# A two-layer hybrid trunk on one core: last states left out, transposed token factors, an ordered end, and sums of squares in two exact passes

## The chip, the cores and the metric

The kernel runs on one core of a Trainium2 chip. The metric is the device time of one execution in microseconds (us). Engines: PE does the matmuls and transposes, DVE and ACT the elementwise work, POOL a few masks, SP issues most transfers.

## What is computed

Two pre-norm residual layers over 1024 tokens of 1024 features, and a last norm. Layer 0 mixes with a convolution branch and an mLSTM with four heads, layer 1 with gated linear attention (GLA), and each is followed by a SwiGLU FFN.

```python
def rmsnorm(x, g):
    return x * rsqrt(mean(x * x, -1) + EPS) * g

def reference(x, ...):
    for l in range(2):
        h = rmsnorm(x, mix_norm_g[l])
        x = x + (conv_mlstm_mixer(h, ...) if l % 2 == 0 else gla_mixer(h, ...))
        h = rmsnorm(x, ffn_norm_g[l])
        x = x + (silu(h @ w1[l]) * (h @ w3[l])) @ w2[l]
    return rmsnorm(x, final_norm_g)

# both recurrent mixers go over chunks of tokens; a chunk reads the state and then renews it
# mLSTM: S = (q k') * decays;  h = (S v + q C) / max(|...|);  C, n = decay * (C, n) + (wk' v, sum wk)
# GLA:   o = A v + (q exp(b)) S;                              S = exp(a) * S + (k exp(a - b))' v
# the convolution branch ends in silu(layernorm(u))
```

## The kernel before

Features lie on the partitions, in 8 tiles of 128, and tokens on the free axis, in two halves of 512. Every large product is `mm3` (L156): both operands are split into a high part, rounded to fp32r, and the rest, also fp32r (`split`, L136: a copy on ACT, L137, and a subtraction on DVE, L138; L152 and L153 do the same for weights in `weights`), and three passes on PE (L158 low weights or low data, L159, L160) make up one fp32 product. The FFN's products are done with seven instead of eight block products, named T1 to T4 and B11 to B22. PSUM has four banks of the tag "mm" and four of "sm".

The instructions on each engine are put in order by a scheduler, when the program is built, from the order of the code and from priorities; `behind(a, b)` (L140) makes a come after b on its engine. In the first mixer the code is emitted in the order of the list `ORDER0`: "a3a" is the preparation (`head_pre`) of head 3 on the first half, "x2b" the mix (`head_mix`) of head 2 on the second half, and so on.

`rstd_half` (L180) makes the reciprocal root of a norm: eight squares on ACT (L185), seven additions on DVE (L187) into `s`, one fp32 matmul with a matrix of 1/1024 (`ones_d`, L189) that sums over the partitions and leaves the result in all of them, and `rsqrt` (ACT L171, DVE L172 to L174). It is called eleven times: twice in the first mixer (`factors`, which also wants the factor of each token on a partition, `rc`: four matmuls of one column, L196, and a second `rsqrt`), after each output projection (twice per layer), after each FFN (L205 then scales), and three times in `finish`, whose last two calls are for 256 tokens each.

`head_pre` loads two rows by SP (`rb`, `wb`), makes the scores (L557), transposes the keys of four chunks (L561), and makes `rb`, `q` and `kw` on DVE (L567, L568, L570). `head_mix` goes over the chunks: L585 the state's increment, L586 and L588 the output, L591 or L594 the new state, L604 the evacuation. In the layer norm of the convolution branch (`layer_norm`, `mean`) four matmuls of 128 columns (L394) add up and sum. In GLA, L799 transposes the keys, L852 makes the increment, L853 and L855 the output, L860 the new state.

The last product, B22, is done in two pieces of 256 tokens. In the second piece the passes go unit by unit (two of the 22 blocks of the inner dimension), the last `LASTU` = 2 units together. L1231 adds the four banks to the residual, and `finish` follows: L1307 scales and L1308 writes out.

Of the kernel before, what the change touches and what calls it, by code (L numbers as in the profile page):

```python
# [29 lines left out]
ORDER0 = ['c0', 'g0', 'c1', 'c2', 'q0', 'c3', 'a0a', 'v0', 'x0a', 'v1', 'x0b', 'g1', 'q1', 'a1a', 'v2', 'x1a', 'v3', 'x1b', 'l', 'g2', 'q2', 'a2a', 'q3', 'x2a', 'x2b', 'a3a', 'n3', 'g3', 'x3a', 'a3b', 'x3b', 'k0', 'n1a', 'n1b']  # L30
# [29 lines left out]
LASTU = 2  # L60
YK = 2
# [11 lines left out]
def trunk_kernel(ctx, tc, xT, cols, gate_b0, ev_vo0, ev_u, ev_cw, ev_out, od_v0, od_u, od_out, gate_w2,  # L73
# [39 lines left out]
    POOL.memset(ones_d, 1.0 / D)  # L113
    epsc = cp.tile([P, 1], F32, tag="epsc", name="epsc")
# [41 lines left out]
    def mm3(o, lt, rt, start, stop, on=False):  # L156

        PE.matmul(o, lt[1], rt[0], start=start and not on, stop=False, skip_group_check=on)  # L158
        PE.matmul(o, lt[0], rt[1], start=False, stop=False, skip_group_check=on)  # L159
        PE.matmul(o, lt[0], rt[0], start=False, stop=stop, skip_group_check=on)  # L160
# [16 lines left out]
    stat = ["sm"]  # L177
    order = [list(range(KT))]

    def rstd_half(xs, r=None, rc=None):  # L180
        n = xs[0].shape[1]
        s = tp.tile([P, HALF], F32, tag="s", name=nm("s"), bufs=1)[:, :n]
        for j, k in enumerate(order[0]):
            q = tmp()[:, :n] if j else s
            ACT.activation(q, xs[k], AF.Square)  # L185
            if j:
                DVE.tensor_tensor(out=s, in0=s, in1=q, op=ALU.add)  # L187
        b = bank(stat[0])[:, :n]
        PE.matmul(b, ones_d, s, start=True, stop=True)  # L189
# [3 lines left out]
        if rc is not None:  # L193
            b = bank("sm")[:, :4]
            for c in range(4):
                PE.matmul(b[:, c:c + 1], s[:, c * P:(c + 1) * P], ones_d[:, 0:1], start=True, stop=True)  # L196
            rsqrt(rc, b)
# [67 lines left out]
    def mixer0(cut, then):  # L265
        with tc.tile_pool(name="m0", bufs=1, reuse_waits="tile") as mp:
# [125 lines left out]
            def mean(b, s):  # L392
                for e in range(4):
                    PE.matmul(b, ones_p, s[:, e * NT:(e + 1) * NT], start=e == 0, stop=e == 3)  # L394
# [151 lines left out]
            def head_pre(hd, half, q, k):  # L546
# [12 lines left out]
                for c in range(4):  # L559
# [4 lines left out]
                for c in range(4):  # L564
# [5 lines left out]
                DVE.tensor_tensor(out=kw.rearrange("p (c t) -> p c t", c=4),  # L570
                                  in0=kb.rearrange("p (c t) -> p c t", c=4),
                                  in1=wk[:, half * 4:half * 4 + 4, hd:hd + 1].to_broadcast([P, 4, P]), op=ALU.mult)
                return q, rb, wb, kw

            def head_mix(hd, half, pre, v, og, st):
                q, rb, wb, kw = pre
                em = gcols["em"]
                for c2 in range(2):
                    db = bank("sm").rearrange("p (c x) -> p c x", c=2)
                    nb = bank("sm").rearrange("p (c x) -> p c x", c=2)  # L580
                    for cc2 in range(2):
# [3 lines left out]
                        PE.matmul(db[:, cc2, :129], kw[:, cs], v[half][:, c, :], start=True, stop=True)  # L585
# [3 lines left out]
                        new = mp.tile([P, 129], F32, tag=f"st{hd % 2}", name=nm("st"), bufs=2)  # L589
                        if st is None:  # L590
                            DVE.tensor_copy(new, db[:, cc2, :129])  # L591
                        else:
# [78 lines left out]
    def mixer1(h, cut, then):  # L671
        y = [[None, None] for _ in range(KT)]
        with tc.tile_pool(name="m1", bufs=1, reuse_waits="tile") as mp:
# [109 lines left out]
            def head_mix(hd, half, q, k, v, st):  # L783
# [8 lines left out]
                kt = tmp()  # L792
                kt3 = kt.rearrange("p (c t) -> p c t", c=4)
# [643 lines left out]
```

## Time and profile before

| | |
|---|---|
| median of 3 runs | 2171.84 us (2170.99 to 2172.52) |
| the profiled execution | 2171.36 us, its span 2169.6 us |
| PE busy | 2152.9 us, 99% |
| DVE busy | 1545.4 us, 71% |
| ACT busy | 866.3 us, 40% |
| granted clock of PE, mean | 0.998 |

The span is what the profiler saw of the program; the execution's own time has 1.76 us around it. A busy PE is not a PE at its peak: records of pipelined matmuls overlap, so the pace of a group is taken from the starts of its first and last instruction. In rows of the timeline the brackets give the idle time of the engine before a row, and what ended it.

### The profile page before, as it was taken

The page shows a single profiled execution, that of the slowest core. Times are in us where ns is not written, and L with a number is a line of the kernel's source. Part 1 is how long each engine was busy: PE and PEld are TensorE (multiplying, and loading weights), DVE is VectorE, ACT ScalarE, POOL GpSimd, SP SyncE. Part 2 cuts the span into 40 slices and gives each one's busy share as a digit, 9 for nine tenths or more (in the row PEclk, how much of TensorE's full clock was granted, in tenths as well). Part 3 has the DMA queues.
Part 4 walks back from the last instruction along what each step waited for, and adds up shares of the span by engine and source line. Part 5 has one row for each costly group of instructions (what it writes and reads, how often), then busy time and mean ns, then how long its engine had stood idle before and what let it go on. Part 6 is the DMA issues. An engine that isn't in the chain of part 4 may idle for free.

```text
span 2169.6 us, 28952 instructions
## 1 busy us (share of the span) xinstructions
PE 2152.9 (99%) x10854; PEld 1830.4 (84%) x10854; DVE 1545.4 (71%) x2585; ACT 866.3 (40%) x1419; POOL 20.8 (1%) x56
## 2 busy tenths in 40 slices
PE   9999999999999999999999999999999999999998
PEld 8889988888888888888889989888888888888887
DVE  7555788777776666867866747587877666667687
ACT  6302327443222323444564534454522222235553
POOL 0000000000000000000110000000000000000000
PEclk9999999999999999999999999999999999999999
DMA  4233453654442336535311011154544333274344
GB/s 167 79 125 111 135 136 117 208 181 170 164 139 95 107 109 211 199 117 165 120 54 40 21 48 31 38 160 170 194 147 165 135 107 107 88 265 157 98 122 131
DMA packets 137979, 278.49 MB, mean 128 GB/s; under 512 B 22320, under 2 KB 35504, under 8 KB 137840
## 3 DMA queue, kind: packets, MB, share of 16 engines
q1 hardware_dynamic: 136688, 275.61, 39.0%
q8 instruction: 85, 1.39, 0.3%
q10 hardware_dynamic: 1152, 1.05, 0.1%
q14 instruction: 54, 0.44, 0.1%
HBM read 209.99 MB, written 66.62 MB: 127 GB/s over the span
## 4 chain that ended last, share of the span: by engine, by line
PE 95%; DVE 3%; ACT 1%; issue 0%; DMA 0%; SPq 0%; DVEq 0%; ACTq 0%
PE mm L158 20%; PE mm L160 20%; PE mm L159 20%; PE sm L159 9%; PE sm L160 9%; PE sm L158 9%; PE sm L382 2%; PE sm L835 1%; PE sm L852 1%; PE sm L853 1%; PE sm L855 1%; PE sm L189 0%; DVE wL L153 0%; PE sm L808 0%; ACT hH L137 0%
## 5 line engine op out<-in xcount | busy, mean ns | idle before, releaser
L159 PE MATMUL mm<-hL,wH 128*128 128x512 f32 x1420 | 555.6, 391 | 0.5 <-DVE hL L310 0.5
L160 PE MATMUL mm<-hH,wH 128*128 128x512 f32 x1420 | 555.3, 391 | 0.0
L158 PE MATMUL mm<-hH,wL 128*128 128x512 f32 x1420 | 520.7, 393 | 1.4 <-DVE wL L153 0.9
L158 PEld LDWEIGHTS mm<-hH,wL 128*128 128x128 f32 x1420 | 266.4, 188 | 58.0 <-DVE wL L153 1.8
L159 PEld LDWEIGHTS mm<-hL,wH 128*128 128x128 f32 x1420 | 266.7, 188 | 55.8 <-DVE hL L310 1.1
L160 PEld LDWEIGHTS mm<-hH,wH 128*128 128x128 f32 x1420 | 266.7, 188 | 54.8
L159 PE MATMUL sm<-hL,wH 128*128 128x512 f32 x616 | 240.5, 390 | 0.0
L160 PE MATMUL sm<-hH,wH 128*128 128x512 f32 x616 | 239.7, 389 | 0.0
L158 PE MATMUL sm<-hH,wL 128*128 128x512 f32 x616 | 209.3, 390 | 0.0
L137 ACT ACTIVATE wH<-S 128x1024 fp32r<-128x1024 f32 x88 | 93.3, 1060 | 212.7 <-PE sm L160 212.7
L137 ACT ACTIVATE wH<-q 128x512 fp32r<-128x512 f32 x143 | 90.4, 632 | 180.4 <-PE mm L160 100.0
L138 DVE TENSOR_TENSOR wL<-q,wH 128x512 fp32r<-128x512 f32 x143 | 98.5, 689 | 73.8 <-ACT wH L137 73.3
L159 PE MATMUL mm<-wL,hH 128*128 128x256 f32 (+2 forms) x512 | 145.8, 286 | 0.0
L160 PE MATMUL mm<-wH,hH 128*128 128x256 f32 (+2 forms) x512 | 145.4, 286 | 0.0
L158 PE MATMUL mm<-wH,hL 128*128 128x256 f32 (+2 forms) x512 | 144.5, 286 | 0.6 <-DVE xy L1231 0.6
L159 PEld LDWEIGHTS sm<-hL,wH 128*128 128x128 f32 x616 | 115.6, 188 | 24.9 <-issue 1.0
L158 PEld LDWEIGHTS sm<-hH,wL 128*128 128x128 f32 x616 | 115.6, 188 | 24.5 <-PE mm L160 0.5
L160 PEld LDWEIGHTS sm<-hH,wH 128*128 128x128 f32 x616 | 115.6, 188 | 24.5 <-issue 0.5
L152 ACT ACTIVATE wH<-raw 128x1024 fp32r<-128x1024 f32 (+2 forms) x77 | 81.6, 1059 | 113.9 <-PE mm L160 84.7
L138 DVE TENSOR_TENSOR wL<-S,wH 128x1024 fp32r<-128x1024 f32 x88 | 107.4, 1220 | 23.9 <-ACT wH L137 23.9
L1040 DVE TENSOR_TENSOR c<-sm,c 128x512 f32<-128x512 f32 x110 | 75.5, 687 | 66.1 <-PE sm L160 66.1
L153 DVE TENSOR_TENSOR wL<-raw,wH 128x1024 fp32r<-128x1024 f32 (+2 forms) x77 | 94.1, 1222 | 38.7 <-ACT wH L152 38.7
(301 smaller groups left out, 3722.2 us busy)
## 6 DMA issues: line engine op xcount, KB each, us to landing
raw<-in_w SPq DMA_DIRECT2D x108, 512.0 KB
mdT<-c SPq DMA_DIRECT2D x88, 256.0 KB
m<-mdT SPq DMA_DIRECT2D x88, 256.0 KB
mdB<-c SPq DMA_DIRECT2D x66, 256.0 KB
q<-in_w SPq DMA_DIRECT2D x60, 256.0 KB
m<-mdB SPq DMA_DIRECT2D x55, 256.0 KB
xsp<-xy SPq DMA_DIRECT2D x48, 256.0 KB
raw<-in_od_u SPq DMA_DIRECT2D x22, 512.0 KB
```

Source lines behind the costliest of these rows:

```text
L137: ACT.activation(dst[0], src, AF.Copy)
L138: return lo.tensor_tensor(out=dst[1], in0=src, in1=dst[0], op=ALU.subtract)
L152: ACT.activation(hi, raw, AF.Copy)
L153: lo.tensor_tensor(out=low, in0=raw, in1=hi, op=ALU.subtract)
L158: PE.matmul(o, lt[1], rt[0], start=start and not on, stop=False, skip_group_check=on)
L159: PE.matmul(o, lt[0], rt[1], start=False, stop=False, skip_group_check=on)
L160: PE.matmul(o, lt[0], rt[0], start=False, stop=stop, skip_group_check=on)
L382: PE.matmul(o, w[:, m * P:(m + 1) * P], raw[:, e, m:m + NT], start=m == 0, stop=m == SH)
L835: PE.matmul(lb[:, j * P:(j + 1) * P], X[:, 2 * j * P:(2 * j + 1) * P], X[:, (2 * j + 1) * P:(2 * j + 2) * P], start=True, stop=True)
L852: PE.matmul(db[:, cc, :], kw[:, cs], v[:, c, :], start=True, stop=True)
L853: PE.matmul(ob[:, cc, :], A[:, cs], v[:, c, :], start=True, stop=st is None)
L1040: DVE.tensor_tensor(out=out, in0=a, in1=b, op=ALU.add)
```

## The change

- `PARTS`: five of the nine sums of squares over 512 tokens (the second of `factors`, the first of layer 0's output projection, both after layer 0's FFN, the first of layer 1's output projection) split `s` (ACT copy, DVE subtraction) and take two fp32r passes with `ones_r`, a copy of `ones_d`, since 1/1024 has no low part.
- `rc`: the result `r`, alike in all partitions, is transposed four times on PE, and one DVE copy takes a column of each.
- `mean`: two additions on DVE (256 and 128 wide) and one matmul, in place of four matmuls; twice.
- Last states: the last chunk of a sequence renews its state for nobody. Its key transposes, increments and state updates are left out in both mixers, four heads each.
- `ORDER0`: "a3a" goes ahead of "x2b", and "a3b" ahead of "x3a".
- Ordered end: in the last two units of the last piece the passes are chained, so that a bank has its nine passes in a row. The scalings of the first piece (`spread`) are put behind later units (`QK` = 6 on). In the last call of `rstd_half` the last square isn't added on DVE: PE sums `s` and that square in two fp32 matmuls.

```diff
-ORDER0 = [..., 'x2a', 'x2b', 'a3a', 'n3', 'g3', 'x3a', 'a3b', 'x3b', 'k0', 'n1a', 'n1b']
+ORDER0 = '... x2a a3a x2b n3 g3 a3b x3a x3b k0 n1a n1b'.split()
+QK = 6
+PARTS = (1, 2, 4, 5, 6)
+    ones_r = cp.tile([P, P], F32R, tag="ones_r", name="ones_r")
+    ACT.activation(ones_r, ones_d, AF.Copy)
...
     def rstd_half(xs, r=None, rc=None):
...
-            if j:
+            if j and (j < KT - 1 or not stat[1]):
                 DVE.tensor_tensor(out=s, in0=s, in1=q, op=ALU.add)
         b = bank(stat[0])[:, :n]
-        PE.matmul(b, ones_d, s, start=True, stop=True)
+        if n < HALF or len(sums) not in PARTS:
+            PE.matmul(b, ones_d, s, start=True, stop=not stat[1])
+            if stat[1]:
+                PE.matmul(b, ones_d, q, start=False, stop=True)
+        else:
+            p = tmp(F32R), tmp(F32R)
+            split(p, s, DVE)
+            PE.matmul(b, ones_r, p[1], start=True, stop=False)
+            PE.matmul(b, ones_r, p[0], start=False, stop=True)
+        sums.append(s)
...
         if rc is not None:
-            b = bank("sm")[:, :4]
+            b = bank("sm")
             for c in range(4):
-                PE.matmul(b[:, c:c + 1], s[:, c * P:(c + 1) * P], ones_d[:, 0:1], start=True, stop=True)
-            rsqrt(rc, b)
+                PE.transpose(b[:, c * P:(c + 1) * P], r[:, c * P:(c + 1) * P], ident)
+            DVE.tensor_copy(rc, b.rearrange("p (c t) -> p c t", c=4)[:, :, 0])
...
             def mean(b, s):
-                for e in range(4):
-                    PE.matmul(b, ones_p, s[:, e * NT:(e + 1) * NT], start=e == 0, stop=e == 3)
+                for n in (2 * NT, NT):
+                    DVE.tensor_tensor(out=s[:, :n], in0=s[:, :n], in1=s[:, n:2 * n], op=ALU.add)
+                PE.matmul(b, ones_p, s[:, :NT], start=True, stop=True)
...
# head_pre of the first mixer; the product kw is n chunks wide too
-                for c in range(4):
+                n = 4 - half
+                for c in range(n):
                     PE.transpose(kb[:, cs], k[:, cs], ident)
...
# head_mix of the first mixer
-                        PE.matmul(db[:, cc2, :129], kw[:, cs], v[half][:, c, :], start=True, stop=True)
+                        more = ci < 7
+                        if more:
+                            PE.matmul(db[:, cc2, :129], kw[:, cs], v[half][:, c, :], start=True, stop=True)
...
-                        else:
+                        elif more:
                             DVE.scalar_tensor_tensor(out=new, in0=st, scalar=wb[:, te:te + 1], ...)
...
# head_mix of GLA: kt, kb and kw have n = 4 - half chunks, and
-                        PE.matmul(db[:, cc, :], kw[:, cs], v[:, c, :], start=True, stop=True)
+                        if c < n:
+                            PE.matmul(db[:, cc, :], kw[:, cs], v[:, c, :], start=True, stop=True)
...
-                        else:
+                        elif c < n:
                             DVE.scalar_tensor_tensor(out=new, in0=st, scalar=ea[:, c:c + 1], ...)
...
# ffn_down
-                            if (name == "B22" or name == "T1" and ks[0] >= SK) and spread:
+                            if (name == "B22" and (not c0 or ks[0] >= QK) or name == "T1" and ks[0] >= SK) and spread:
                                 for ins in spread.pop(0):
                                     behind(ins, low)
+                        if final and c0 and ks[-1] == N - 1:
+                            while spread:
+                                for ins in spread.pop(0):
+                                    behind(ins, low)
...
+                    prev = []
                     for i in range(4):
                         for k, w, m in g:
-                            mm3(banks[i], wcol(w, i, P), m, k == 0, k == N - 1, on)
+                            ins = mm3(banks[i], wcol(w, i, P), m, k == 0, k == N - 1, on)
+                            if len(us) > 1:
+                                for m_ in ins:
+                                    if prev:
+                                        behind(m_, prev[-1])
+                                    prev = [m_]
...
-                    stat[0] = "sm" if half else "mm"
+                    stat[:] = "sm" if half else "mm", final and c0 > 0
```

Where instructions stand: rows of one engine in program order, with the line, the operation and out<-in by the program's names. Line numbers of the kernel after are larger (L162 to L164 are the three passes, L606, L607 and L609 are L585, L586 and L588, L643 is L622).

PE at the first sum of the first mixer, before (`mm_...` are the input projections):

```order
L159 MATMUL mm_272<-hL_40_181,wH_120 128x512
L160 MATMUL mm_272<-hH_39_180,wH_120 128x512
L189 MATMUL sm_208<-s_185,ones_d 128x512
L196 MATMUL sm_215<-ones_d,s_185 128x1 x4
L334 MATMUL sm_265<-e_263 128x128
L159 MATMUL mm_326<-hL_55_227,wH_117 128x512
```

After; the transposes of `rr` stand 46 passes behind the sum:

```order
L164 MATMUL mm_270<-hH_39_182,wH_122 128x512
L196 MATMUL sm_210<-s_187,ones_d 128x512
L163 MATMUL mm_324<-hL_54_225,wH_119 128x512
L164 MATMUL mm_324<-hH_53_224,wH_119 128x512
...
L163 MATMUL mm_349<-hL_68_253,wH_122 128x512
L164 MATMUL mm_349<-hH_67_252,wH_122 128x512
L212 MATMUL sm_217<-ident,rr_186 128x128 x4
L350 MATMUL sm_263<-e_261 128x128
L162 MATMUL mm_442<-wH_425,hL_26_155 128x264
```

The token factors moved from directly behind the sum to the end of the following projections, in front of the small matmul of L350 (L334 before).

PE at the end of head 3 in the first mixer, before; `uw` are weights of the next stage's product, `mm_3478` an output projection:

```order
L160 MATMUL mm_3580<-hH_541_3416,uw_3574 128x512
L561 MATMUL sm_3328<-ident,qk_2895 128x128 x4
L585 MATMUL sm_3342<-v_3053,kw_3340 128x129
L586 MATMUL sm_3343<-v_3053,rb_3319 128x129
L588 MATMUL sm_3343<-st_3307,qk_2859 128x129
L586 MATMUL sm_3343<-v_3053,rb_3319 128x129
L585 MATMUL sm_3364<-v_3053,kw_3340 128x129
L586 MATMUL sm_3365<-v_3053,rb_3319 128x129
L585 MATMUL sm_3342<-v_3053,kw_3340 128x129
L588 MATMUL sm_3343<-st_3347,qk_2859 128x129
L588 MATMUL sm_3365<-st_3352,qk_2859 128x129
L586 MATMUL sm_3365<-v_3053,rb_3319 128x129
```

After, with head 3's second preparation some 50 rows earlier:

```order
L574 MATMUL sm_3265<-qk_2848,qk_2884 128x128 x4
L579 MATMUL sm_3270<-ident,qk_2884 128x128 x3
L606 MATMUL sm_3283<-v_3037,kw_2956 128x129
L162 MATMUL mm_3459<-hH_525_3367,wL_3454 128x512
...
L609 MATMUL sm_3305<-st_3309,qk_2776 128x129
L607 MATMUL sm_3327<-v_3038,rb_3261 128x129
L609 MATMUL sm_3327<-st_3314,qk_2848 128x129
L607 MATMUL sm_3327<-v_3038,rb_3261 128x129
L606 MATMUL sm_3348<-v_3038,kw_3281 128x129
L606 MATMUL sm_3326<-v_3038,kw_3281 128x129
L609 MATMUL sm_3327<-st_3331,qk_2848 128x129
L607 MATMUL sm_3349<-v_3038,rb_3261 128x129
```

The transposes moved ahead of the products of the next stage; the row of small matmuls at the end now has the first half's last chunk in it and no product between.

PE at the end of the kernel, before; `mm_18474` to `mm_18477` are the four banks:

```order
L158 MATMUL mm_18477<-hH_3414_18611,q_18403 128x256
L159 MATMUL mm_18474<-hL_3415_18612,q_18403 128x256
L160 MATMUL mm_18474<-hH_3414_18611,q_18403 128x256
L159 MATMUL mm_18475<-hL_3415_18612,q_18403 128x256
L160 MATMUL mm_18475<-hH_3414_18611,q_18403 128x256
L159 MATMUL mm_18476<-hL_3415_18612,q_18403 128x256
L160 MATMUL mm_18476<-hH_3414_18611,q_18403 128x256
L159 MATMUL mm_18477<-hL_3415_18612,q_18403 128x256
L160 MATMUL mm_18477<-hH_3414_18611,q_18403 128x256
L189 MATMUL sm_18678<-s_18655,ones_d 128x256
```

After, the last bank and the sum:

```order
L162 MATMUL mm_18462<-hH_3411_18590,q_18351 128x256
L163 MATMUL mm_18462<-hL_3412_18591,q_18351 128x256
L164 MATMUL mm_18462<-hH_3411_18590,q_18351 128x256
L162 MATMUL mm_18462<-hH_3411_18590,q_18355 128x256
...
L163 MATMUL mm_18462<-hL_3415_18597,q_18388 128x256
L164 MATMUL mm_18462<-hH_3414_18596,q_18388 128x256
L196 MATMUL sm_18662<-s_18640,ones_d 128x256
L198 MATMUL sm_18662<-t_18660,ones_d 128x256
```

The last two passes of each bank moved in front of the next bank's passes, and the sum is two matmuls.

DVE ahead of that, before (`hL_3415` is the low half of the last operand):

```order
L1307 SCALAR_TENSOR_TENSOR xy_3004_16787<-xy_3004_16787,col,r_18452 128x256
L1307 SCALAR_TENSOR_TENSOR xy_3066_17039<-xy_3066_17039,col,r_18452 128x256
L1307 SCALAR_TENSOR_TENSOR xy_3068_17043<-xy_3068_17043,col,r_18452 128x256
L1307 SCALAR_TENSOR_TENSOR xy_3070_17047<-xy_3070_17047,col,r_18452 128x256
L1307 SCALAR_TENSOR_TENSOR xy_3072_17051<-xy_3072_17051,col,r_18452 128x256
L187 TENSOR_TENSOR s_18655<-s_18655,t_18663 128x256
L138 TENSOR_TENSOR hL_3415_18612<-m_18609,hH_3414_18611 128x256
L1231 TENSOR_TENSOR xy_2998_16775<-xy_2998_16775,mm_18474 128x256
L1231 TENSOR_TENSOR xy_3000_16779<-xy_3000_16779,mm_18475 128x256
L1231 TENSOR_TENSOR xy_3002_16783<-xy_3002_16783,mm_18476 128x256
L1231 TENSOR_TENSOR xy_3004_16787<-xy_3004_16787,mm_18477 128x256
L187 TENSOR_TENSOR s_18655<-s_18655,t_18666 128x256
```

After:

```order
L1341 SCALAR_TENSOR_TENSOR xy_3004_16772<-xy_3004_16772,col,r_18437 128x256
L193 TENSOR_TENSOR s_18640<-s_18640,t_18648 128x256
L142 TENSOR_TENSOR hL_3415_18597<-m_18594,hH_3414_18596 128x256
L1341 SCALAR_TENSOR_TENSOR xy_3066_17024<-xy_3066_17024,col,r_18437 128x256
L1341 SCALAR_TENSOR_TENSOR xy_3068_17028<-xy_3068_17028,col,r_18437 128x256
L1341 SCALAR_TENSOR_TENSOR xy_3070_17032<-xy_3070_17032,col,r_18437 128x256
L1341 SCALAR_TENSOR_TENSOR xy_3072_17036<-xy_3072_17036,col,r_18437 128x256
L1265 TENSOR_TENSOR xy_2998_16760<-xy_2998_16760,mm_18459 128x256
L1265 TENSOR_TENSOR xy_3000_16764<-xy_3000_16764,mm_18460 128x256
L193 TENSOR_TENSOR s_18640<-s_18640,t_18651 128x256
L1265 TENSOR_TENSOR xy_3002_16768<-xy_3002_16768,mm_18461 128x256
L193 TENSOR_TENSOR s_18640<-s_18640,t_18654 128x256
L193 TENSOR_TENSOR s_18640<-s_18640,t_18657 128x256
```

The low half moved ahead of four scalings, and the squares' sums stand between the adds of the banks.

More of the change, by code (lines that the diff above doesn't have):

```diff
@@ L156, in mm3 @@
     def mm3(o, lt, rt, start, stop, on=False):
-        PE.matmul(o, lt[1], rt[0], start=start and not on, stop=False, skip_group_check=on)
-        PE.matmul(o, lt[0], rt[1], start=False, stop=False, skip_group_check=on)
-        PE.matmul(o, lt[0], rt[0], start=False, stop=stop, skip_group_check=on)
+        return (PE.matmul(o, lt[1], rt[0], start=start and not on, stop=False, skip_group_check=on),
+                PE.matmul(o, lt[0], rt[1], start=False, stop=False, skip_group_check=on),
+                PE.matmul(o, lt[0], rt[0], start=False, stop=stop, skip_group_check=on))
     def wcol(w, k, c):
@@ L791, in head_mix @@
                 DVE.tensor_tensor(out=qt, in0=qt, in1=q, op=ALU.mult)
[L792 to L794 removed]
+                n = 4 - half
+                kt = tmp()[:, :n * P]
+                kt3 = kt.rearrange("p (c t) -> p c t", c=n)
+                DVE.tensor_tensor(out=kt3, in0=b3[:, :n, P - 1:P].to_broadcast([P, n, P]), in1=b3[:, :n], op=ALU.subtract)
                 ACT.activation(kt, kt, AF.Exp, scale=1.0 / 16)
[L796 to L798 removed]
+                DVE.tensor_tensor(out=kt, in0=kt, in1=k[:, :n * P], op=ALU.mult)
+                kb = bank("sm")[:, :n * P]
+                for c in range(n):
                     PE.transpose(kb[:, c * P:(c + 1) * P], kt[:, c * P:(c + 1) * P], ident)
[L800 removed]
+                kw = mp.tile([P, HALF], F32, tag="kw", name=nm("kw"), bufs=1)[:, :n * P]
                 ACT.activation(kw, kb, AF.Copy)
```

22 lines of the change are left out of this document (9 added, 13 removed).

## The prediction

> **What bounds the kernel now.** I read the head of the page first, then the chain of waits, then the stretches of the timeline that the edits touch.
>
> ```profile
> span 2169.6 us, 28952 instructions
> PE 2152.9 (99%) x10854; PEld 1830.4 (84%) x10854; DVE 1545.4 (71%) x2585; ACT 866.3 (40%) x1419; POOL 20.8 (1%) x56
> PEclk9999999999999999999999999999999999999999
> PE 95%; DVE 3%; ACT 1%; issue 0%; DMA 0%; SPq 0%; DVEq 0%; ACTq 0%
> ```
>
> PE is busy 99% of the span and carries 95% of the chain, and its clock is at 9 in every slice. So nearly everywhere a matmul taken away shortens the run by its own pace, unless DVE or ACT then becomes late. Two places differ: the last 12 us, where PE waits for the last norm, and the first mixer, where DVE is nearly as full as PE. The sum is made against the profiled execution, which took 2171.36 us (1.76 us around its span); the median of the three runs, 2171.84, stands 0.48 above it.
>
> **Prices.** The pieces of the chain in order of time give what an instruction costs when PE is the bound. The columns are start, length, what, and number of records; an fp32 matmul leaves two records, an fp32r pass or a transpose one.
>
> ```profile
> 243.67 0.44 PE sm L561 x4
> 256.96 0.89 PE sm L394 x8
> 876.80 0.91 PE mm L158 x4
> 1088.42 0.86 PE sm L189 x2
> 1159.45 0.44 PE sm L799 x4
> 1179.77 0.43 PE sm L852 x2
> ```
>
> - Sums of squares: one fp32 matmul 512 wide is 0.86; an fp32r pass of that width is 0.91/4 = 0.227, two are 0.455. Five sums: 5 x (0.86 - 0.455) = 2.0 us less.
> - Factors of the tokens:
>
> ```profile
> 19.42 1.02 PE L189 MATMUL sm<-s,ones_d 128*128 128x512 f32 x2
> 20.28 0.95 PE L196 MATMUL sm<-ones_d,s 128*128 128x1 f32 x8
> 21.15 0.48 PE L334 MATMUL sm<-e 8*128 8x128 f32 x2
> ```
>
> From the start of the four one-column matmuls to the next is 21.15 - 20.28 = 0.87; four transposes are 0.44 (row 243.67). Twice: 0.9 us less.
> - Mean and variance of the layer norm: four accumulating matmuls, 0.89, become one, 0.22: twice 0.67 = 1.3 us less.
> - Last states: 4 transposes of L561 at 0.11 = 0.44; 4 matmuls of L585 at 0.22 (taken as L394, 128 against 129 columns) = 0.89; 4 transposes of L799 at 0.11 = 0.44; 4 matmuls of L852 at 0.43 = 1.7.
>
> Together 7.7 us of PE. Of these 3.9 lie in the first mixer (one sum 0.4, factors 0.9, mean 1.3, L561 0.4, L585 0.9), and 3.8 outside (four sums 1.6, GLA 2.1).
>
> **Outside the first mixer.** The state updates that go there free DVE as well, so 2.1 passes whole. Each split sum puts a copy and a subtraction between the added squares and PE: 1.3 us by 24 splits that have 512 columns too.
>
> ```profile
> L138 DVE TENSOR_TENSOR hL<-t,hH 128x512 fp32r<-128x512 f32 x24 | 15.9, 681 | 0.0
> L137 ACT ACTIVATE hH<-t 128x512 fp32r<-128x512 f32 x24 | 15.0, 627 | 1.3 <-DVE t L205 1.1
> ```
>
> The tightest of the four is the sum at 1088.42, where the second half of layer 1 waits for it.
>
> ```profile
> 1092.46 3.40 DVE L205 SCALAR_TENSOR_TENSOR t<-xy,col,r 128x512 f32<-128x512 f32 x5
> 1098.09 0.60 PE L739 MATMUL sm<-ident,glc 128*128 128x128 f32 x4
> ```
>
> PE has 9.7 us of other matmuls from that sum to row 1098.09, and DVE starts the scaling at 1092.46; a scale that comes 1.2 later can cost between 0 and 1.2. I take 0: in the new order the two passes stand behind 13 more matmuls of the first half (1.6 us), and 39 are left between them and the work that needs the norm. If this cover were gone, the late one would be the subtraction that feeds the second half's first projection. The copy of the constant (ACT, once, at the start) falls where ACT waits for the first weights: nothing.
>
> **The end.** Rows by engine, with the idle time and its releaser in brackets:
>
> ```profile
> 2147.43 0.60 PE L189 MATMUL sm<-s,ones_d 128*128 128x256 f32 x2
> 2153.90 0.42 DVE L138 TENSOR_TENSOR hL<-m,hH 128x256 fp32r<-128x256 f32 x1
> 2157.45 0.28 PE L160 MATMUL mm<-hH,q 128*128 128x256 f32 x1
> 2157.05 1.41 DVE L1231 TENSOR_TENSOR xy<-xy,mm 128x256 f32<-128x256 f32 x4 [2.74 <-PE mm L160]
> 2158.39 2.00 DVE L187 TENSOR_TENSOR s<-s,t 128x256 f32<-128x256 f32 x4
> 2157.57 1.41 ACT L185 ACTIVATE t<-xy 128x256 f32<-128x256 f32 x4 [6.58 <-DVE xy L1231]
> 2160.45 1.22 PE L189 MATMUL sm<-s,ones_d 128*128 128x256 f32 x2 [2.71 <-DVE s L187]
> 2161.70 0.47 ACT L171 ACTIVATE r<-sm,epsc 128x256 f32<-128x256 f32 x1 [2.73 <-PE sm L189]
> ```
>
> And two windows (us, busy PE, PEld, DVE, ACT, POOL, granted clock, DMA share, GB/s):
>
> ```profile
> 2157.00:2160.00 3.00, 0.73 (x7) 0.53 (x5) 2.63 (x8) 1.41 (x4) 0.00 (x0) 0.96 0.00 0
> 2160.00:2162.00 2.00, 1.22 (x2) 0.51 (x2) 0.39 (x1) 0.30 (x1) 0.00 (x0) 0.50 0.00 0
> ```
>
> Before, the four banks are finished 0.24 apart, so four adds, four squares and four sums form a tail of 3 us (2157.45 to 2160.45). Afterwards each bank takes its nine matmuls in a row, 9 x 0.12 = 1.08 us, so banks 0 to 2 are added, squared and summed under PE. After the last matmul there remain: the third bank's sum, which DVE has queued ahead of the last add (it ends near 2158.1: bank 2 done 1.08 earlier, then 0.32 to its add, 0.52 to its square, 0.47 to its sum, each with its length); the last add; its square 0.52 later, 0.42 long; then PE's second matmul near 2159.1. That is 1.35 earlier. DVE must have the last low half (row 2153.90) before PE's eighth matmul of the row of 36 rather than its 29th: that is due near 2154.1, and in the new order only four of the eight scalings stand ahead of it instead of all eight, so it ends near 2152.7. If that failed, PE would wait 0.2 at most by the old time.
>
> The second piece of the gain is the clock. The last sum takes 1.22 at a granted clock of 0.50, and the same shape at 2147.43 takes 0.60. PE had stood still 2.71 us. With two matmuls in place of one, PE pauses only some 0.4 us before each, so I take 0.60: 0.6 us more. Low end: 0 (the clock drops anyway); the first of the two matmuls is hidden, since the last square is ready only later. The end gives 2.0 us, at least 1.3. By the Trainium skill ("TensorE: Matmul & The Clock Gate", Part 1) the clock follows how busy the PE has recently been over a window of about 3.4 us; no row here measures that length, and by it a pause of 0.4 us could not halve the clock.
>
> **The first mixer.** Windows of 20 us, then PE's waits in the last of them, then two DVE rows ahead of the first wait:
>
> ```profile
> 280.00:300.00 20.00, 20.00 (x97) 16.77 (x95) 19.15 (x33) 5.20 (x6) 0.00 (x0) 1.00 0.35 96
> 330.00:350.00 20.00, 20.00 (x164) 19.61 (x163) 19.00 (x42) 19.94 (x37) 0.00 (x0) 1.00 0.28 81
> 350.00:370.00 20.00, 17.88 (x108) 15.22 (x107) 16.91 (x41) 10.88 (x36) 0.00 (x0) 1.00 0.47 142
> ```
>
> ```profile
> 351.89 0.49 PE L585 MATMUL sm<-v,kw 128*128 128x129 f32 x2 [0.70 <-DVE st L591]
> 353.02 0.50 PE L158 MATMUL mm<-hH,wL 128*128 128x512 f32 x1 [0.42 <-DVE wL L153]
> 364.56 0.49 PE L585 MATMUL sm<-v,kw 128*128 128x129 f32 x2 [0.78 <-DVE kw L570]
> 366.84 0.49 PE L588 MATMUL sm<-st,qk 128*128 128x129 f32 x2 [0.22 <-DVE st L594]
> ```
>
> ```profile
> 349.30 2.08 DVE L138 TENSOR_TENSOR hL<-xy,hH 128x512 fp32r<-128x512 f32 x2
> 351.55 0.28 DVE L591 COPY st<-sm 128x129 f32<-128x129 f32 x1
> ```
>
> PE can run ahead of DVE only by what DVE has free: 0.85 us in the window from 280, 1.00 in that from 330, together 1.85. What is saved behind 350 us (half of L561 and L585, 0.66) meets a DVE that has 3 us free. So of 3.9 us 1.85 + 0.66 = 2.5 pass. DVE's own work hardly changes: 1.4 us of narrow adds at most (four, each no longer than the 0.35 of an add 256 wide in row 2157.05), 0.7 for a split, against four state updates of 0.28 and six operations of the second reciprocal root taken out.
>
> The new order puts head 3's preparation (its two row loads on SP, the scores, transposes, exponentials and DVE's three products) ahead of head 2's second mix. That takes the wait for kw (0.78) away, since some 50 passes then lie between kw's product and its use, and leaves other work between the first matmuls of head 3's first half, where PE now waits 0.70 for a state copy queued behind a split of 2.08. PE is idle 20.00 - 17.88 = 2.1 us there. Its bounds: 2.1 gained, or 2.1 lost, if the preparation delays a split by as much as the split in row 349.30 delays the state. The loads cost nothing with a DMA share of 0.28. I take 1.0 gained: the two waits for head 3's state are replaced by a bare row of 14 small matmuls at the end, in which matmul, state update and next matmul follow one another; row 366.84 shows such a link waiting 0.22, and four or five links are 1 us.
>
> **Sum.** Outside 3.8, end 2.0, first mixer 2.5, waits 1.0: 9.3 us. 2171.36 - 9.3 = 2162.1 for the profiled execution, 2162.5 for the median.
>
> **Rivals.**
> - The first mixer swallows its part: DVE or ACT (19.94 of 20 in the window from 330) sets the pace there, and nothing of 2.5 + 1.0 arrives. 2171.84 - 5.8 = 2166.0, and 2168.1 if the new order loses 2.1. For it speak the full windows; against it that PE does not wait inside them.
> - The waits go completely and the whole 3.9 passes: 3.8 + 2.0 + 3.9 + 2.1 = 11.8, 2160.0. For it: each of the four waits has one releaser that the change moves or takes out.
> - The end gains only its 1.35, at a clock of 0.50: 2163.1.
> - Transposes that are dearer than the matmuls they replace. A transpose by itself lasts 0.27 (row 1098.09: 0.60 less three paces of 0.11). If eight of them did not overlap, they would cost 2.2 in place of 1.74, and 1.3 of the sum would be gone: 2163.8. The rows of L561 and L799 speak against it, at 0.11 each. The Trainium skill (the same page, Part 4) gives about 275 ns for a transpose and says that full clock does not engage for it; the trace agrees with the length of one and disagrees on the clock, which is at 9 in every slice, and on the pace.
> - Slower: the bare row at the end of head 3. With no product left to cover it, each pair of chunks goes through state update, next matmul, and the drain of its output bank on DVE. It decides if the idle time there grows from 2.1 to more than 9.3 - 1.0 + 2.1 + 4.3 = 14.7 us, that is over 1 us for each of its 14 matmuls against 0.22 in row 366.84.
>
> **How the numbers follow.** A measurement of this kernel tells about 0.2% (4.3 us) from no change: faster is below 2167.5, slower above 2176.2. My forecast, including the small variants of clock and transposes (0.05 each): 0.55, between 2160.7 and 2164.5. Waits gone: 0.17. First mixer swallowed: 0.25, of which 0.10 lies above 2167.5. Slower: 0.03. The range from 2159 (all gained, and 1 us of further waits) to 2167.5 leaves out the 0.10, the 0.03 and some 0.04 below. Faster 0.55 + 0.17 + 0.15 = 0.87, same 0.10, slower 0.03.
>
> **What would show it.** PE busy about 7.7 us less or a little more. Two passes of some 0.45 in place of 0.86 at the five sums, with no wait at the one near 1085. Four transposes at 0.44 near 30 us. In the window from 350, less than 1.2 us of idle PE, and no wait for kw. At the end the adds 1.08 us apart, the last sum about 1.4 after the last matmul starts plus 0.2, and a granted clock of 1.00 there. I am wrong if waits of several us stand between 330 and 380, or if PE waits for the last low half before its final 36 matmuls.

## The result, and the profile after

The changed kernel takes 2160.07 us (median of 4 runs, 2159.46 to 2161.12) against 2171.41 us (2170.93 to 2172.52): 11.3 us less, a ratio of 0.9948 with a 95% interval of 0.9932 to 0.9964. The forecast was 2162.5. Its profiled execution took 2160.24 us. The head of its page:

```profile
span 2158.3 us, 28864 instructions
PE 2145.6 (99%) x10812; PEld 1827.2 (85%) x10812; DVE 1543.7 (72%) x2581; ACT 867.8 (40%) x1423; POOL 22.9 (1%) x56
...
PE 98%; DVE 1%; DMA 0%; ACT 0%; issue 0%; SPq 0%; DVEq 0%; ACTq 0%
```

PE is busy 7.3 us less, and carries 98% of the chain instead of 95%: what went beside the 7.3 was time in which PE stood idle (16.7 us before, 12.7 after). DVE's busy time is nearly what it was (1543.7 against 1545.4).

Where the 11.3 us went is read by following one kind of instruction through both traces. There are 3172 third passes (L160, L164 after; the last of the three passes of a product); the table has the start of some, counted from 0. Around the order's change a pass and its namesake are not the same product, so only places behind it are compared.

| third pass | before | after | difference | what lies since the row above |
|---|---|---|---|---|
| 0 | 7.52 | 8.08 | +0.56 | the first loads (ACT's first input 0.31 later) |
| 15 | 19.19 | 19.83 | +0.64 | PE at half its pace for longer |
| 544 | 382.90 | 378.94 | -3.96 | the first mixer |
| 1620 | 1104.83 | 1099.50 | -5.33 | three split sums |
| 2140 | 1479.51 | 1471.58 | -7.93 | GLA |
| 2200 | 1522.91 | 1513.73 | -9.18 | the split sum of layer 1's output projection |
| 3171, the last | 2157.45 | 2148.23 | -9.22 | nothing |
| end of span | 2169.6 | 2158.3 | -11.3 | the end: 2.1 |

At the start PE of the changed kernel runs at half its pace until 10.2 us. Two rows of it, then two of before at the same time; the starts are 0.43 and 0.23 apart:

```profile
9.37 0.63 PE L163 MATMUL mm<-hL,wH 128*128 128x512 f32 x1
9.80 0.63 PE L164 MATMUL mm<-hH,wH 128*128 128x512 f32 x1
```

```profile
9.06 0.39 PE L158 MATMUL mm<-hH,wL 128*128 128x512 f32 x1
9.29 0.39 PE L159 MATMUL mm<-hL,wH 128*128 128x512 f32 x1
```

The prices of the new instructions, from the chain in order of time:

```profile
31.56 0.43 PE sm L212 x4
...
274.61 0.22 PE sm L411 x2
...
1085.15 0.23 PE sm L203
1085.38 0.23 PE sm L204
```

Transposes 0.43 for four, one mean 0.22, two passes 0.46: the rows answer to the prices of the prediction. The window and PE's only named wait of the stretch that lost 2.1 us before, with the DVE rows ahead of it:

```profile
330.00:350.00 20.00, 19.15 (x152) 18.46 (x151) 18.93 (x41) 19.80 (x38) 0.00 (x0) 1.00 0.41 107
350.00:370.00 20.00, 19.60 (x109) 16.62 (x110) 16.87 (x43) 10.49 (x36) 0.00 (x0) 1.00 0.55 158
```

```profile
350.22 0.50 PE L162 MATMUL mm<-hH,wL 128*128 128x512 f32 x1 [1.07 <-DVE wL L157]
```

```profile
347.69 1.09 DVE L142 TENSOR_TENSOR hL<-xy,hH 128x512 fp32r<-128x512 f32 x1
348.70 0.34 DVE L532 TENSOR_SCALAR v<-mm,rt 128x128 f32<-128x128 f32 x1
348.96 1.21 DVE L157 TENSOR_TENSOR wL<-raw,wH 128x1024 fp32r<-128x1024 f32 x1
```

Idle PE between 330 and 370 is 0.85 + 0.40 = 1.25 us instead of 2.1. The wait for kw and that for the state copy are gone; the wait for the split weights (0.42 before) has grown to 1.07, behind a full DVE.

And the end, PE and DVE:

```profile
2148.23 0.28 PE L164 MATMUL mm<-hH,q 128*128 128x256 f32 x1
2148.86 0.70 PE L196 MATMUL sm<-s,ones_d 128*128 128x256 f32 x2 [0.35 <-DVE s L193]
2149.70 0.70 PE L198 MATMUL sm<-t,ones_d 128*128 128x256 f32 x2
```

```profile
2145.31 0.42 DVE L1265 TENSOR_TENSOR xy<-xy,mm 128x256 f32<-128x256 f32 x1 [0.22 <-PE mm L164]
2146.39 0.42 DVE L1265 TENSOR_TENSOR xy<-xy,mm 128x256 f32<-128x256 f32 x1 [0.66 <-PE mm L164]
2147.47 0.42 DVE L1265 TENSOR_TENSOR xy<-xy,mm 128x256 f32<-128x256 f32 x1 [0.32 <-PE mm L164]
2148.38 0.43 DVE L193 TENSOR_TENSOR s<-s,t 128x256 f32<-128x256 f32 x1
2148.72 0.41 DVE L1265 TENSOR_TENSOR xy<-xy,mm 128x256 f32<-128x256 f32 x1
```

The adds stand 1.08 apart, and the last is held back by the third bank's sum, by 0.17 only. From the start of the last pass to the end it is 10.07 us instead of 12.12. Of these 2.05 us, 0.52 is the clock of one execution: the last sum took 1.22 at a clock of 0.50 before and takes 0.70 now, and in six other traces of the old end it took 0.70 as well (see e6_warm).

### The profile page after: what moved, and what is told of

The parts are those of the page before. It is cut to its first block, busy times and chain, and to the rows that moved or that the text cites. A ratio compares the mean times of both kernels' runs of the same rounds, so it can differ in the third digit from the quotient of the medians.

```text
span 2158.3 us, 28864 instructions
## 1 busy us (share of the span) xinstructions
PE 2145.6 (99%) x10812; PEld 1827.2 (85%) x10812; DVE 1543.7 (72%) x2581; ACT 867.8 (40%) x1423; POOL 22.9 (1%) x56
## 4 chain that ended last, share of the span: by engine, by line
PE 98%; DVE 1%; DMA 0%; ACT 0%; issue 0%; SPq 0%; DVEq 0%; ACTq 0%
PE mm L162 21%; PE mm L163 21%; PE mm L164 21%; PE sm L163 9%; PE sm L164 9%; PE sm L162 9%; PE sm L398 2%; PE sm L858 1%; PE sm L877 1%; PE sm L876 1%; PE sm L879 1%; PE sm L607 0%; PE sm L831 0%; PE sm L906 0%; PE sm L574 0%; PE sm L609 0%
## 5 line engine op out<-in xcount | busy, mean ns | idle before, releaser
L164 PE MATMUL mm<-hH,wH 128*128 128x512 f32 x1420 | 555.4, 391 | 0.0
L162 PE MATMUL mm<-hH,wL 128*128 128x512 f32 x1420 | 520.8, 393 | 1.7 <-DVE wL L157 1.1
L162 PEld LDWEIGHTS mm<-hH,wL 128*128 128x128 f32 x1420 | 267.2, 188 | 57.6 <-ACT hH L325 1.6
L164 PEld LDWEIGHTS mm<-hH,wH 128*128 128x128 f32 x1420 | 267.2, 188 | 54.8 <-issue 0.2
L164 PE MATMUL sm<-hH,wH 128*128 128x512 f32 x616 | 240.0, 390 | 0.0
L162 PE MATMUL sm<-hH,wL 128*128 128x512 f32 x616 | 209.1, 391 | 0.0
L162 PE MATMUL mm<-wH,hL 128*128 128x256 f32 (+2 forms) x512 | 145.5, 288 | 0.6 <-DVE xy L1265 0.6
L164 PE MATMUL mm<-wH,hH 128*128 128x256 f32 (+2 forms) x512 | 145.8, 286 | 0.0
L162 PEld LDWEIGHTS sm<-hH,wL 128*128 128x128 f32 x616 | 115.7, 188 | 24.4 <-PE mm L164 0.5
L164 PEld LDWEIGHTS sm<-hH,wH 128*128 128x128 f32 x616 | 115.7, 188 | 24.2 <-issue 0.2
```

The source lines that it names most:

```text
L162: return (PE.matmul(o, lt[1], rt[0], start=start and not on, stop=False, skip_group_check=on), PE.matmul(o, lt[0], rt[1], start=False, sto ...
```

## The experiments

Each kernel was timed in five rounds against the kernel before. The intervals of the ratios are about +-0.001 (2 us), so differences under 2 us rest on the traces: on the table's kind of comparison, since apart from its first 20 us and the clock at its end a trace mostly repeats to a few tenths.

**The ordered end alone** (e1_end): all other parts of the diff undone.

> The kernel before with the ordered end alone (chained passes, scalings behind later units, last sum in two matmuls). My forecast's theory: 2.0 us less than before (1.35 because the adds, squares and sums of three banks run under PE, 0.6 because the clock stays at 1.00), and nothing changed ahead of the last 12 us. Rival, the clock drops as before: 1.35 us less, with a granted clock of 0.50 at the last matmul. Third theory, the chained passes make PE wait for the last low half: a wait before the last 36 passes, and less than 1 us of gain.

2170.02 us, ratio 0.9994 (0.9985 to 1.0003). From the last pass (2157.98) to the end of the span it is 10.06 us, 2.06 less than before, as in the changed kernel. The median shows 1.6, which fits what this end gains on the other traces of the old one (1.5, see e6_warm). In this trace PE was also 0.6 later from 178 us on, where a later split of weights pushed `kw` behind.

**The same with one sum on PE** (e5_chain):

```diff
-                    stat[:] = "sm" if half else "mm", final and c0 > 0
+                    stat[:] = "sm" if half else "mm", False
```

> The ordered end alone, but the last square is added on DVE again and PE sums once. Theory that the granted clock follows PE's pause: PE now stands still some 1.8 us between its last pass and the sum (0.35 and 0.3 with two matmuls, 2.71 in the kernel before). If a pause of that length is already enough, the sum takes 1.2 us at 0.50 and the run is about 1 us below the kernel before; if not, it takes 0.6 to 0.7 at 1.00, and the gain is about 1.6. Rival, the length of the sum has nothing to do with the pause: 1.2 us as in the kernel before.

2170.14 us, ratio 0.9993 (0.9984 to 1.0002); from the last pass (2157.12) to the end 10.53 us.

```profile
2159.05 0.70 PE L196 MATMUL sm<-s,ones_d 128*128 128x256 f32 x2 [1.64 <-DVE s L193]
```

```profile
2159.00:2160.00 1.00, 0.70 (x2) 0.30 (x2) 0.00 (x0) 0.21 (x1) 0.00 (x0) 1.00 0.00 0
```

With a pause of 1.64 the clock is still at 1.00. The sum starts 1.93 behind the last pass instead of 3.00. So of the 2.05 us at the end the chained banks bring 1.1 by hiding adds, the second matmul 0.5, and 0.5 is the length of the sum.

**PE kept at work in the old end** (e6_warm):

```diff
             ACT.activation(q, xs[k], AF.Square)
+            if len(stat) > 2 and stat[2] and j >= 4:
+                warm = warm if j > 4 else bank("sm")
+                PE.matmul(warm[:, :n], ones_d, q, start=True, stop=True)
...
+                    stat[:] = "sm" if half else "mm", False, final and c0 > 0
```

> The kernel before with four matmuls more: PE also sums each of the last four squares by itself into a bank that nobody reads, while DVE adds them. It does no useful work, and only fills PE's pause of 2.7 us in front of the last sum (to about 0.4 ahead of them and under 1 behind). If the clock drops because PE pauses: the last sum takes 0.6 to 0.7 at a granted clock of 1.00 in place of 1.22 at 0.50, and the run is 0.5 to 0.6 us shorter in spite of the added work. Rival (the sum is slow for another reason): 1.2, no gain, or a loss.

2171.86 us, ratio 1.0001 (0.9992 to 1.0010). The sum:

```profile
2161.25 0.70 PE L199 MATMUL sm<-s,ones_d 128*128 128x256 f32 x2 [0.41 <-DVE s L196]
```

0.70 in place of 1.22, at 1.00, and 11.58 us from the last pass (2158.26) to the end, 0.54 less than before; this trace is 0.8 later by third pass 15, and the whole run gained nothing that could be measured. The sum came out as expected, but this does not show that the added work held the clock. Six other traces have the old end without it (e2_mixer, e3_order, e8_parts, e9_gla, e10_dve_load, e13_dve_early), with the same pause, and in each the sum takes 0.70. The row of e2_mixer:

```profile
2156.34 0.70 PE L196 MATMUL sm<-s,ones_d 128*128 128x256 f32 x2 [2.71 <-DVE s L193]
```

From the last pass to the end they take 11.58 to 11.90 us, with no gain left for the added matmuls. So the sum of 1.22 belongs to one execution of the kernel before: a pause of 2.71 us does not by itself halve the clock, and against these traces the ordered end is worth 1.5 to 1.8 us, not 2.05. None of six traces of the chained end has a slow sum, against one of seven of the old end; whether the new end makes it rarer is not shown.

**What leaves PE work out of the first mixer, alone** (e2_mixer): `PARTS = (1,)`, the factors, the mean and the first mixer's last states; the old order.

> The kernel before with only what leaves PE work out of the first mixer: the second sum split, factors transposed, one matmul for the mean, last states dropped; the old order of emission, 3.9 us of PE. My forecast's theory (DVE paces the stretch from 280 to 350 us): 2.5 us less than before, and more idle PE between 350 and 370 than the 2.1 of before. Rival (PE is the bound everywhere there): 3.9 us less, with idle PE about as before.

2167.22 us, ratio 0.9981 (0.9972 to 0.9990): 4.4 us less. Third pass 391 (276.67 before) is 3.5 earlier, pass 544 and the last 4.1; 0.2 of this is an earlier start. The rival holds: all of it passes, and most is in hand before the full stretch begins. The waits of PE keep their sizes (0.79, 0.42, 0.65, 0.22; before 0.70, 0.42, 0.78, 0.22) and stand 3.5 to 3.8 earlier, and idle PE in the two windows from 330 to 370 is 1.21 + 0.87 = 2.1, as before.

**More DVE work late** (e10_dve_load), on top of e2_mixer; it is in the trace between 302 and 365 us:

```diff
+                if hd > 1:
+                    for _ in range(2):
+                        DVE.tensor_tensor(out=extra, in0=q, in1=wb, op=ALU.mult)
                 kw = mp.tile([P, HALF], F32, tag="kw", name=nm("kw"), bufs=KB)
```

> The kernel of the first mixer's savings alone (2167.2 us) with eight products more on DVE, 512 wide, two in each preparation of heads 2 and 3, into a tile that nobody reads: 8 x 0.6 = 4.9 us of DVE work between about 260 and 365 us. If DVE paces that stretch, as my forecast had it: 3 to 5 us more. If PE paces it and DVE only has little free in single windows: less than 1 us more, with waits of PE for DVE near 350 somewhat longer.

2171.27 us, 4.05 more than without. PE's waits, and two windows:

```profile
349.63 0.49 PE L611 MATMUL sm<-v,kw 128*128 128x129 f32 x2 [1.51 <-DVE st L617]
351.82 0.47 PE L162 MATMUL mm<-hH,wL 128*128 128x512 f32 x1 [1.47 <-DVE wL L157]
```

```profile
348.00:352.00 4.00, 1.02 (x7) 0.73 (x6) 4.00 (x7) 2.99 (x9) 0.00 (x0) 1.00 0.35 75
352.00:356.00 4.00, 4.00 (x12) 3.10 (x12) 3.62 (x11) 2.28 (x6) 0.00 (x0) 0.57 0.88 260
```

Up to third pass 500 (343 us) nothing is lost against e2_mixer; by pass 544 it is 3.2. About 1.5 of that is idle PE (1.88 + 1.69 in the two windows of 20 us against 2.1), the rest a granted clock near 0.50 for some 3.4 us behind it. So DVE has little to spare near 350, as my forecast said, and sets the pace there once work is added. That it sets the pace without added work is not shown; e2_mixer speaks against it.

**More DVE work early** (e13_dve_early): the same eight products with `if hd < 2`, in the trace from 151 to 248 us.

> As the run with eight more products on DVE, but in the preparations of heads 0 and 1, which lie ahead of 250 us, where DVE is busy half to three quarters of the time. If what matters is how full DVE is at that place: within 0.5 us of the first mixer's savings alone, 2167.2. If DVE is full over the whole first mixer, so that added work always comes out at its end: 3 to 4 us more, as in the late place.

2167.23 us, against 2167.22 without them: nothing. The 4.9 us vanish where DVE has room:

```profile
120.00:180.00 60.00, 59.78 (x401) 54.58 (x401) 33.34 (x62) 10.27 (x26) 0.00 (x0) 1.00 0.50 158
180.00:240.00 60.00, 59.78 (x425) 55.69 (x424) 33.60 (x76) 12.70 (x41) 0.00 (x0) 1.00 0.38 123
```

**The new order alone** (e3_order), and **all but the new order** (e4_old_order):

> The kernel before with the new order of emission alone. My forecast's theory: 1.0 us less, since the wait for kw and that for the state copy go and a bare row at the end of head 3 costs about 1. Rival, all waits go: 2.1 us less. Third theory, the order only moves the waits: within 0.3 us of before, with as much idle PE between 330 and 370 us as before.

> The changed kernel with the old order of emission. If the order is worth 1.0 us as forecast: 1.0 us more than the changed kernel, 2161.1. If all waits go by it: 2.1 more, 2162.2. If it only moves waits: 2160.1, the same. If the order is what lets the removed work of the first mixer pass: 1.4 more on top of the 1.0, 2162.5.

Alone 2170.33 us, ratio 0.9994 (0.9985 to 1.0003), 1.3 less by medians and 1.3 by third pass 544. Idle PE from 330 to 370 is 0.65, with two waits for split weights:

```profile
352.31 0.50 PE L162 MATMUL mm<-hH,wL 128*128 128x512 f32 x1 [0.32 <-DVE wL L157]
356.46 0.50 PE L162 MATMUL mm<-hH,wL 128*128 128x512 f32 x1 [0.22 <-DVE wL L157]
```

Without it 2161.0 us, ratio 0.9952 (0.9940 to 0.9965): 0.9 more than the changed kernel by medians. By the traces it is 0.7: e4_old_order runs 0.74 ahead of the changed kernel from third pass 15 to 391, by its start alone, and 0.06 ahead at pass 544. The forecast's 1.0 is near in both. The order doesn't make the savings pass: e4_old_order is 4.0 ahead of before at pass 544 too.

**The split sums alone** (e8_parts) and **GLA's last states alone** (e9_gla):

> The kernel before with the five split sums alone. By the price of the passes: 5 x 0.41 = 2.0 us less, and one more 0.5 to 0.6 if the wait for the low weights that follows the first sum of layer 1's output projection (0.47 in the kernel before) goes by it, as it is gone in the changed kernel. Rival: the copy and subtraction ahead of the sum cost a wait at the sum near 1088, and the gain is 0.8 to 1.2.

> The kernel before with GLA's last states alone dropped. By price 2.16 us less. Rival, the vector engine sets the pace in GLA: more than 2.2 (the state updates and narrower products there free it too) if PE waited for it, less than 1.5 if the output evacuations do.

2169.52 us, ratio 0.9990 (0.9982 to 0.9999), and 2168.35 us, ratio 0.9987 (0.9978 to 0.9996). By third passes the split sums bring 0.1 (the second of `factors`), 0.45, 0.5, 0.4 and, at layer 1's output projection, 1.2. There the sum is 0.4, and the wait of 0.47 that stood behind it goes (0.7 at its place), since the order of DVE's work has turned about. Before, the eight scalings stood ahead of the weights' split; with the split sum, one split stands ahead of the end of the root:

```profile
1490.05 5.39 DVE L942 SCALAR_TENSOR_TENSOR xy<-xy,col,r 128x512 f32<-128x512 f32 x8
1495.35 1.28 DVE L248 TENSOR_TENSOR xy<-xy,mm 128x512 f32<-128x512 f32 x2
1496.55 1.22 DVE L153 TENSOR_TENSOR wL<-raw,wH 128x1024 fp32r<-128x1024 f32 x1
```

```profile
1491.64 1.22 DVE L157 TENSOR_TENSOR wL<-raw,wH 128x1024 fp32r<-128x1024 f32 x1
1492.77 0.69 DVE L178 SCALAR_TENSOR_TENSOR r<-t,r 128x512 f32<-128x512 f32 x1
```

GLA brings 2.5 between third passes 1620 and 2140, 0.4 more than its price; no wait of PE is named there before or after, and where the 0.4 lies was not settled.

The five parts alone, by medians: 1.6 + 4.4 + 1.3 + 1.7 + 2.9 = 11.9, of which 0.1 to 0.4 is counted twice (the second sum is in two of them): 11.5 to 11.8, against 11.3 for all together. They add up, as far as medians good to about 2 us each can tell.

**All nine sums split** (e7_all_parts):

```diff
-PARTS = (1, 2, 4, 5, 6)
+PARTS = range(9)
```

> The changed kernel with all nine sums over 512 tokens split, the four that the change leaves whole too (the first of the first mixer, the second of each output projection, the first half of the last norm). PE work falls by 4 x 0.41 = 1.6 us. If cover is at hand there as well: 1.6 us less than the changed kernel, 2158.4. If the copy and subtraction (1.3 us) stand on the path where the next matmuls wait for that norm: a wait of up to 1.3 behind each, so between 1.6 less and 3.6 more than the changed kernel (4 x 0.9).

2165.57 us, ratio 0.9971 (0.9959 to 0.9982): 5.5 more than the changed kernel, beyond my range.

```profile
27.89 0.39 PE L203 MATMUL sm<-t,ones_r 128*128 128x512 f32 x1
...
33.94 1.09 PE L212 MATMUL sm<-ident,rr 128*128 128x128 f32 x4 [3.62 <-DVE rr L178]
```

The first sum, at 20.06 in the changed kernel, now comes at 27.89: its split stands on ACT and DVE among the splits of the first inputs, and everything in the mixer waits for it. By third pass 72 this one has cost 5.4 against the changed kernel, and 6.2 without the difference at the start. The idle time of 3.62 is only part of it: the clock fell behind this pause, and PE worked at half clock from 33.9 to 40.2, about 3 us more:

```profile
34.00:40.00 6.00, 6.00 (x25) 5.45 (x26) 5.90 (x12) 4.27 (x7) 0.00 (x0) 0.50 0.59 175
```

My range had allowed a wait of 1.3 and no change of the clock. Of the other three sums, the first half of the last norm gains 0.4, the two second halves of the output projections 0.1 each.

**Two scalings off DVE, and the last norm's first sum split** (e12_pool8), on top of the changed kernel:

```diff
-PARTS = (1, 2, 4, 5, 6)
+PARTS = (1, 2, 4, 5, 6, 8)
...
+            if half and c0 and k in (4, 5):
+                ACT.activation(t, t, AF.Copy, scale=c1(C_FIN + k))
+                POOL.tensor_tensor(out=t, in0=t, in1=r, op=ALU.mult)
+            else:
                 work.append([DVE.scalar_tensor_tensor(out=t, ...
```

> The changed kernel with one more sum split (the first half of the last norm, the one of the four that lost nothing when split), and two of the last eight scalings taken off DVE: ACT multiplies by the column ahead of time, and POOL by the root. Two scalings less on DVE's last chain are 0.8 us, the split 0.4: 1.2 us less than the changed kernel, 2158.9, if POOL does its two within the 2.4 us that DVE needs for six. Rival, a product 128x256 on POOL takes over 1.2 us, or slows DVE: no gain at the end, 2159.7 or more.

2159.74 us, ratio 0.9948 (0.9935 to 0.9960), as the changed kernel. DVE and POOL at the end:

```profile
2151.31 3.40 DVE L1345 SCALAR_TENSOR_TENSOR xy<-xy,col,r 128x256 f32<-128x256 f32 x6
```

```profile
2151.45 1.79 POOL L1343 TENSOR_TENSOR xy<-xy,r 128x256 f32<-128x256 f32 x2 [698.02 <-DVE r L178]
```

POOL needs 0.9 for each, within its time, but DVE then takes 3.40 for six, where it took 3.26 for eight: the end is 0.2 longer. The six are not all slower (shortest, median and longest in ns):

```profile
L1345 DVE SCALAR_TENSOR_TENSOR xy<-xy,col,r x6: 472/479/948, 2151.3 to 2154.2; 128x256 f32<-128x256 f32 x6
```

Two of them take 0.94 to 0.95 us each, about as long as the two products of POOL beside them; the other four take 0.47 to 0.49, as all eight do in the changed kernel.

## Why the prediction came out as it did

The direction and the prices held, and the time lay in the range; the size was 9.3 forecast against 11.3, near the rival in which the waits go and all savings pass (2160.0). Some of the closeness is luck: in the profiled pair two things that the change did not cause nearly cancel, the later start (0.64) and the slow sum of the kernel before (0.52). Without both, the traces give 4.6 for the first mixer and the order, 5.3 outside and 1.5 at the end: 11.4. By its steps:

- Prices: right. 7.7 us priced, PE busy 7.3 less. The rival of dearer transposes is out: four in a row take 0.43 of the chain. The clock digit of a slice of 54 us, to which the forecast pointed, could not tell the clock of a row of 0.44 us; the row's length can: four transposes have 0.53 to the next start at 1.00 (31.40 in the changed kernel) and 1.01 at 0.50 (33.94 in e7_all_parts).
- Outside the first mixer, 3.8: too small by 1.4. 1.4 + 2.6 + 1.25 = 5.2 measured. GLA gave 0.4 more; the rest is mainly the wait of 0.47 at layer 1's output projection and what hung on it, a row in the trace of before that I had not read for this change. No wait came at the sum near 1085: taking 0 between 0 and 1.2 was right.
- The end, 2.0: met in the profiled pair at 2.05, partly by luck. The last matmul starts 1.53 earlier against the last pass (1.35 forecast: 1.1 by hiding and 0.5 by the second matmul). The other term, 0.6 for the clock, came from a single execution: the forecast took the sum of 1.22 at 0.50 for the result of PE's 2.71 us of rest, and six other traces have that rest with a sum of 0.70. Against them the clock's term is 0 and the end gains 1.5 to 1.8. Tying it to the two matmuls was wrong too, since one sum also kept the clock (e5_chain).
- The first mixer, 2.5 of 3.9: wrong. All passes (4.1 in e2_mixer, 0.2 of it the start). The step that failed is "PE can run ahead of DVE only by what DVE has free: 0.85 in the window from 280, 1.00 in that from 330". DVE's little room does bound work that is added to it inside such a stretch, as e10_dve_load shows; whether it bounds PE's work saved inside one was not tested. But most of the saving (3.5) arises ahead of 280, where DVE has room (29.66 of 40 us busy from 240 to 280 before, 32.14 in e2_mixer). DVE's work then starts earlier as well, and the full stretch moves as a whole: PE's wait behind DVE's state copy at 351.89 stands at 348.35 in e2_mixer.
- The new order, 1.0: right (1.3 alone; on top 0.9 by medians, 0.7 by the traces). Its reason was half right: the waits for kw and the state went, but what came in their place was not the bare row of 14 matmuls. That row loses at most 0.6 in the chain (two pieces about 0.25 longer than their like, and a gap of 0.08); the price is the wait for split weights, 1.07.
- Not foreseen: a start 0.56 later in the profiled execution, 0.64 by third pass 15. The kernels with the same first instructions show -0.2 to +0.8 at that pass, and two that hold the change too (e4_old_order, e12_pool8) -0.1 and 0.0, so it is no cost of the change.

## What to carry to other kernels

On an engine that is busy 99%, price each removed instruction by the pace of its neighbours and take it whole, also where another engine is full further on; what is saved ahead of such a stretch moves the stretch. A saving inside the stretch is still to be tested. Test a suspected second bound by adding work to it, once in the full place and once where there is room (here 4.05 us and nothing for the same eight instructions). A cheaper instruction with a longer latency pays where its result is not awaited: the same split sum gave 0.4 to 0.5 at three places and cost 5.4 where a whole mixer waited for it and the clock fell as well. And a slow row of one trace is not yet a cost: look for the same row in other traces before the sum counts on it.

## What the runs showed of the hardware

A pause of PE can be paid for later, and the clock does not react at once. Windows of before, of the single sum (e5_chain), of the changed kernel, and of the late DVE load (e10_dve_load); the clock is the third column from the end:

```profile
2159.75:2160.00 0.25, 0.00 (x0) 0.00 (x0) 0.14 (x2) 0.00 (x0) 0.00 (x0) 0.57 0.00 0
```

```profile
2161.50:2161.75 0.25, 0.00 (x0) 0.00 (x0) 0.21 (x2) 0.00 (x0) 0.00 (x0) 0.58 0.00 0
```

```profile
2153.50:2154.00 0.50, 0.00 (x0) 0.00 (x0) 0.50 (x3) 0.00 (x0) 0.00 (x0) 0.90 0.63 215
```

```profile
352.50:353.00 0.50, 0.50 (x3) 0.37 (x2) 0.50 (x3) 0.00 (x0) 0.00 (x0) 0.60 0.70 156
355.50:356.00 0.50, 0.50 (x3) 0.34 (x2) 0.50 (x4) 0.00 (x0) 0.00 (x0) 0.50 0.95 234
356.00:356.50 0.50, 0.50 (x5) 0.46 (x4) 0.50 (x2) 0.15 (x1) 0.00 (x0) 0.99 0.81 315
```

PE's last record ahead of the fall ends at 2157.73, 2159.75 and 2150.40 in the first three, so the clock fell 2.1, 1.8 and 3.5 us later. In the fourth, PE was idle 3.0 of the 4 us from 348 to 352, was back at work, and the clock fell only then, for about 3.4 us, at an estimated cost of 1.7 (half of it). In e7_all_parts it fell at 33.3, 3.0 us behind the last pass, and stayed at 0.50 until 40.2, though PE was back at work at 33.9. The Trainium skill ("TensorE: Matmul & The Clock Gate", Part 1) describes a free-running activity window of about 3.4 us; the varying delay and the length of the slow stretch, once and twice 3.4 us, agree with it. So the length of a pause does not settle its price: behind the same 2.71 us the sum took 1.22 in one trace and 0.70 in six.

The clock column has a gap at the start: the window from 8 to 10 us of the changed kernel reads 1.00, while its passes start 0.43 apart. And two scalings of 128x256 on DVE took 0.95 in place of 0.48 while POOL's products, 0.9 each, ran beside them; the others kept their time. This looks as if DVE had stood still for part of each, but no run here separates that from other causes.
